# Down products of two SwiGLU layers: eight of 22 row pairs as seven block products in three of the four column halves

## The chip, the cores and the metric

The kernel is one program on one core of one Trainium2 chip. The metric is the device time of one execution in microseconds (us); each kernel is given as the median of its runs.

## What is computed

A decoder layer on a sequence of 256 rows of width 2048, all float32: a half-step SwiGLU, a mixing layer (a recurrent one and a gated linear one side by side), a second half-step SwiGLU, a final norm. The change concerns the two SwiGLU layers alone, and in them the last product, `@ w_down`.

```python
D_FF = 11 * D_MODEL // 4        # 5632
def swiglu(x, w_gate, w_up, w_down):
    return (jax.nn.silu(x @ w_gate) * (x @ w_up)) @ w_down

h = h + 0.5 * swiglu(rms_norm(h, ffn1_norm[l]), ffn1_w_gate[l], ffn1_w_up[l], ffn1_w_down[l])
...                             # mixing layer
h = h + 0.5 * swiglu(rms_norm(h, ffn2_norm[l]), ffn2_w_gate[l], ffn2_w_up[l], ffn2_w_down[l])
return rms_norm(h, final_norm)
```

## The kernel before, in words

Every float32 operand is split into a rounded part and a rest (`hi`, `lo`), and a product is three matmuls: hi by hi, hi by lo, lo by hi (`three`, lines 156 to 158). For a weight the split is made on the fly: one 1 MB transfer, issued by SyncE (line 134), brings a **pair** of row tiles (256 rows by 1024 columns) into a buffer `wst`; ScalarE casts 1024 elements per partition into `whi` (line 116) and VectorE subtracts them into `wlo` (line 117).

The down product of a layer runs over two **pieces**, the column halves of `w_down`. In each piece the 5632 rows of `w_down` are 22 pairs, and `DOWN_PLAN` says in one letter each how a pair is multiplied:

- **n**, plain: two row tiles by two row blocks of the output by two column blocks, 8 block products, 24 matmuls of 512 columns. Two casts and two subtractions of 1024 elements.
- **S**, shared: the 2 by 2 blocks are combined as in Strassen's and Winograd's schemes, 7 block products, 21 matmuls. VectorE first forms sums of weight blocks into a second buffer `t` (lines 143, 144, 145), and then `b11,b21` (one split of 1024), `b22` (one of 512), `t1,t3` and `t2,t4` (1024 each) are split. The sums of the other side, the hidden activations `hT`, are made beforehand (`block_sums`, and `earlier_sums` for pairs whose activations stand early).

Buffers decide how far ahead the weights can be prepared. `wst`, `whi` and `wlo` have three buffers each (pool `wpool`, `bufs=3`), `b22` has one of its own. A buffer is handed out again in turn and is waited for until its last reader is done. In the gate and up products the sums `t` of an S lie in a separate room; in the down products (`core.room = None`) `t` takes one of the three `wst` buffers, so an S takes two of the three. With n, S and t handed out in turn, "nnS" repeated moves the buffers on by one each time, while in "nS" repeated an S gets the buffer of the S before it, and an n that of the n before it.

The order on each engine is fixed when the program is built, by priorities; a row that waits holds up all behind it on that engine, and SyncE issues its transfers in order too.

Of the kernel before, what the change touches and what calls it, by code (L numbers as in the profile page):

```python
# [12 lines left out]
F32 = mybir.dt.float32  # L13
F32R = mybir.dt.float32r
# [3 lines left out]
P = 128  # L18
# [244 lines left out]
        nc.vector.reciprocal(rstd, tmp)  # L263


def ffn(core, xhi, xlo, rstd, wg, wu, wd, after_first, after_down, fpool, down, rest, back, spare, more, head=None):
    nc, NT, NK, D, S = core.nc, core.NT, core.NK, core.D, core.S
    DFF = wg.shape[1]
    NF = DFF // P
# [89 lines left out]
    for c0, w in chunks:  # L359
        if c0:  # L360
            own, aux = ([core.bank(i) for i in b] for b in (range(4), range(4, 8)))
            sg = fpool.tile([P, NT, 1024], F32, name=core.name("sg"), tag="sg")
            last_s = GATE_PLAN.rindex("S")
            hooks = {last_s: [lambda: shared(aux, sg)]}
# [32 lines left out]
        sg = scrap  # L397
# [11 lines left out]
        pending = [lambda c0=c0, w=w, hid=hid: hidden_T(c0, w, hid)]  # L409
    core.room = None  # L410
    back()
    four, (hraw, two) = spare(), more()
    first_s = NF // 2 - 6
    hsums = lambda p: four(p) if p >= NF // 2 - 4 else tuple(two[:, i, p - first_s, :] for i in range(2))

    def earlier_sums():

        for n, p in enumerate(range(first_s, first_s + 2)):
            pair = slice(2 * p, 2 * p + 2)
            nc.vector.tensor_tensor(hraw[:, n], hT_hi[:, pair, :].bitcast(F32), hT_lo[:, pair, :].bitcast(F32), ALU.add)  # L420
            block_sums(hraw[:, n], *hsums(p))

    for piece, (c0, w) in enumerate(down):
        own, aux = ([core.bank((4 * piece + i) % 8) for i in b] for b in (range(4), range(4, 8)))
        plan = DOWN_PLAN[piece]
        number = {"n": iter(range(first_s)), "S": iter(range(first_s, NF // 2))}
        ids = [next(number[kind]) for kind in plan]
        hooks = {}
        if piece == 0:
            hooks[0] = [earlier_sums]  # L430
            hooks[DOWN_HIDDEN_AT] = [partial(f, sums=hsums) for f in pending]
        tmp = lambda: fpool.tile([P, NT, 1024], F32, name=core.name("dsh"), tag="hid")
        hooks[plan.rindex("S")] = [lambda: shared_h(aux, tmp(), c0)]
        core.rows_times_pairs(wd, c0, plan, ids, own, aux, hT_hi, hT_lo, hsums, hooks)
        for n in range(2):
            for t in range(NT):
                hs = core.h[:, t, c0 + n * 512 : c0 + (n + 1) * 512]
                nc.vector.scalar_tensor_tensor(hs, own[2 * t + n], 0.5, hs, ALU.mult, ALU.add)
            after_down(piece, n)
# [676 lines left out]
NSLOT = 17  # L1116
GATE_PLAN, UP_PLAN = "nSnSnSnn", "nSnSnSnn"
HIDDEN_AT = 6
DOWN_PLAN, DOWN_HIDDEN_AT = ("nnnnSnnSnnSnnSnnSnnSnn", "nnSnnSnnSnnSnnSnnSnnnn"), 2


@with_exitstack
def kernel(ctx: ExitStack, tc: tile.TileContext, dram: dict, out: bass.AP):
    nc = tc.nc
    x = dram["x"][0]
    S, D = x.shape
    core = Core(ctx, tc, S, D, 1024)
    const, NK = core.const, core.NK
    HD = D // 2
# [7 lines left out]
    rstd = [const.tile([P, core.NT], F32, name=f"rstd{i}") for i in range(4)]  # L1137
# [8 lines left out]
    def norm_half(i, hf, xhi, xlo):  # L1146
        core.transposed(hf * NK // 2, NK // 2, gT[:, i * NK : (i + 1) * NK], xhi, xlo, (0, 1, 2, 3) if hf == 0 else (4, 5, 6, 7))

    def norm_rows(i, bank, pool):
        for hf in range(2):  # L1150
            core.sumsq(hf * HD, HD, ssq[i][hf], pool)
        core.rstd_of(ssq[i][:2], rstd[i])
        if bank is not None:
            core.spread_rstd(rstd[i], bank)
# [14 lines left out]
    with ExitStack() as front:  # L1169
        xa, xa_half, xa_sums, xa_pool = xt_pool(front, "xa")  # L1170
        with ExitStack() as st:
            hpool = st.enter_context(tc.tile_pool(name="h1", bufs=1))
            fpool = st.enter_context(tc.tile_pool(name="ffn1", bufs=1))
            core.h = hpool.tile([P, core.NT, D], F32, name="h1", tag="h")
            with tc.high_priority(offset=9000):
                load_gain(0, fpool, nc.scalar)
            for q in range(4):
                with tc.high_priority(offset=(9000, 8600, 8400, 8300)[q]):
                    cs = slice(q * 512, (q + 1) * 512)
                    nc.sync.dma_start(out=core.h[:, :, cs], in_=x[:, cs].rearrange("(t p) d -> p t d", p=P))  # L1180

            def norm_quarter(q):
                core.transposed(4 * q, 4, gT[:, :NK], *xa, ((2, 3), (4, 5), (6, 7))[q % 3])

            with tc.high_priority(offset=8800):
                norm_quarter(0)

            def first_norm():
                with tc.issue_after(core.last_split.ins):
                    norm_rows(0, 7, fpool)  # L1190
                for i in (1, 2):
                    load_gain(i, fpool, nc.sync)

            def rest():
                return hpool.tile([P, core.NT, D], F32, name="wsums1", tag="h")

            def back():
                core.h = hpool.tile([P, core.NT, D], F32, name="h1b", tag="h")
                for hf in range(2):
                    cs = slice(hf * HD, (hf + 1) * HD)  # L1200
                    nc.sync.dma_start(out=core.h[:, :, cs], in_=x[:, cs].rearrange("(t p) d -> p t d", p=P))

            def more():

                raw = xa_pool.tile([P, 4, 2, S], F32, name="hsum1", tag="lo0")
                return raw, fpool.tile([P, 2, 2, 512], F32R, name="hsum1b", tag="sg")

            def park(hf, n):
                if n == 0:
                    return  # L1210
                for n, v in zip(("hi", "lo"), xa):
                    v.tiles[hf] = xa_half(n, hf)
                norm_half(1, hf, *xa)
                if hf == 1:
                    norm_rows(1, 6, fpool)
                nc.sync.dma_start(out=parked[hf], in_=core.h[:, :, hf * HD : (hf + 1) * HD])

            ffn(core, *xa, rstd[0], dram["ffn1_w_gate"][0], dram["ffn1_w_up"][0], dram["ffn1_w_down"][0],
                first_norm, park, fpool, [(0, HD), (HD, HD)], rest, back, xa_sums, more, head={q: partial(norm_quarter, q + 1) for q in range(3)})
        mix_layer(core, dram, *xa, scratch, NSLOT)  # L1220
        right = dict(side="right", reuse_waits="tile")
        h2 = ctx.enter_context(tc.tile_pool(name="h2", bufs=1, **right))

        def back2():
            core.h = h2.tile([P, core.NT * D + 24], F32, name=core.name("h2"), tag="h")[:, : core.NT * D].rearrange(
                "p (t d) -> p t d", t=core.NT)
            for hf in range(2):
                nc.sync.dma_start(out=core.h[:, :, hf * HD : (hf + 1) * HD], in_=parked[hf])

        back2()  # L1230
        xb, _, xb_sums, xb_pool = xt_pool(ctx, "xb", **right)

        def half_done(hf):
            norm_half(2, hf, *xb)
            nc.sync.dma_start(out=parked[hf], in_=core.h[:, :, hf * HD : (hf + 1) * HD])

        mix_out(core, dram["w_out"][0], *xa, half_done)
    with ExitStack() as st:
        fpool = st.enter_context(tc.tile_pool(name="ffn2", bufs=1, reuse_waits="tile"))
        down = [(0, HD), (HD, HD)]  # L1240
        fb = None

        def more2():
            raw = xb_pool.tile([P, 4, 2, S], F32, name="hsum2", tag="lo0")
            return raw, xb_pool.tile([P, 2, 2, 512], F32R, name="hsum2b", tag="hi0")

        def closing(piece, n):
            nonlocal fb
            if piece == 0 and n == 0:
                return  # L1250
            if piece == 0:
                with tc.issue_after(core.last_silu.ins):
                    nc.scalar.activation(warm, ssq[0][0], AF.Sqrt)
                fb = fpool.tile([P, D], F32, name="final_gain", tag="sg")
                nc.sync.dma_start(out=fb, in_=dram["final_norm"].rearrange("(o d) -> o d", o=1).broadcast_to([P, D]))
            c0, w = ((0, HD), (HD, HD // 2), (HD + HD // 2, HD // 2))[piece + n * piece]
            core.sumsq(c0, w, ssq[3][piece + n * piece], fpool)
            for t in range(core.NT):
                hs = core.h[:, t, c0 : c0 + w]
                nc.vector.tensor_tensor(hs, hs, fb[:, c0 : c0 + w], ALU.mult)  # L1260

        def rest2():
# [2 lines left out]

        warm = const.tile([P, core.NT], F32, name="warm")
        ffn(core, *xb, rstd[2], dram["ffn2_w_gate"][0], dram["ffn2_w_up"][0], dram["ffn2_w_down"][0],
            lambda: norm_rows(2, 7, fpool), closing, fpool, down, rest2, back2, xb_sums, more2)
        core.rstd_of(ssq[3], rstd[3])
        for hf in range(2):  # L1270
            for t in range(core.NT):
# [34 lines left out]
```

## Time and profile before

| | |
|---|---|
| median of 3 runs | 1915.48 us (1914.80 to 1916.83) |
| profiled execution: its own time | 1916.29 us |
| span of that execution, first to last instruction | 1914.6 us |
| granted TensorE clock, mean | 0.994 of full speed |
| TensorE (PE) busy | 1881.2 us, 98% |
| VectorE (DVE) busy | 1575.3 us, 82% |
| ScalarE (ACT) busy | 1036.2 us, 54% |

The span and the profiled execution's own time differ by 1.7 us, which lies outside the first and last instruction. Times in rows are us from the start of the span. PE rows of matmuls overlap: the distance between two starts is what one costs.

### The profile page before, as it was taken

The page shows a single profiled execution, that of the slowest core. Times are in us where ns is not written, and L with a number is a line of the kernel's source. Part 1 is how long each engine was busy: PE and PEld are TensorE (multiplying, and loading weights), DVE is VectorE, ACT ScalarE, POOL GpSimd, SP SyncE. Part 2 cuts the span into 40 slices and gives each one's busy share as a digit, 9 for nine tenths or more (in the row PEclk, how much of TensorE's full clock was granted, in tenths as well). Part 3 has the DMA queues.
Part 4 walks back from the last instruction along what each step waited for, and adds up shares of the span by engine and source line. Part 5 has one row for each costly group of instructions (what it writes and reads, how often), then busy time and mean ns, then how long its engine had stood idle before and what let it go on. Part 6 is the DMA issues. An engine that isn't in the chain of part 4 may idle for free.

```text
span 1914.6 us, 25771 instructions
## 1 busy us (share of the span) xinstructions
PE 1881.2 (98%) x10161; PEld 1583.4 (83%) x10161; DVE 1575.3 (82%) x2044; ACT 1036.2 (54%) x1261; POOL 9.6 (1%) x53
## 2 busy tenths in 40 slices
PE   7999999999999999999999999999999999999997
PEld 6888888888888889898899978888878888888886
DVE  6889899898978776986595775988898989987876
ACT  6555555655555555543454554665655555554553
POOL 0000000000000001000000000000000000000000
PEclk9999999999999999998999999999999999999999
DMA  6556555655556566545243456655655555656664
GB/s 224 194 188 208 179 214 181 215 187 210 199 199 227 203 204 213 179 122 152 79 145 118 126 200 204 206 209 178 217 179 200 195 198 197 240 185 203 213 204 141
DMA packets 124401, 360.77 MB, mean 188 GB/s; under 512 B 20879, under 2 KB 23128, under 8 KB 124152
## 3 DMA queue, kind: packets, MB, share of 16 engines
q1 hardware_dynamic: 123960, 358.08, 55.6%
q8 instruction: 79, 1.29, 0.3%
q10 hardware_dynamic: 320, 1.06, 0.1%
q14 instruction: 42, 0.34, 0.1%
HBM read 351.25 MB, written 7.86 MB: 188 GB/s over the span
## 4 chain that ended last, share of the span: by engine, by line
PE 89%; DVE 5%; DMA 3%; ACT 2%; issue 1%; SPq 0%; DVEq 0%; ACTq 0%
PE bank L157 21%; PE bank L158 21%; PE bank L156 21%; PE bank L205 4%; PE bank L206 4%; PE bank L207 4%; PE bank L196 3%; PE bank L194 3%; PE bank L193 3%; DMA wst<-in_ffn_w_up_dram 2%; DVE wlo L117 1%; DVE wlo L98 1%; PE bank L286 1%; PE bank L781 1%; DMA wst<-in_ffn_w_gate_dram 1%
## 5 line engine op out<-in xcount | busy, mean ns | idle before, releaser
L116 ACT CAST whi<-wst 128x1024 fp32r<-128x1024 f32 (+1 forms) x544 | 528.6, 987 | 419.5 <-PE bank L158 374.4
L117 DVE TENSOR_TENSOR wlo<-wst,whi 128x1024 fp32r<-128x1024 f32 (+1 forms) x544 | 610.0, 1137 | 87.6 <-ACT whi L116 78.9
L157 PE MATMUL bank<-wlo,hThi 128*128 128x512 f32 x824 | 322.1, 391 | 1.7 <-DVE wlo L117 1.7
L156 PE MATMUL bank<-whi,hThi 128*128 128x512 f32 x824 | 320.8, 389 | 0.0
L158 PE MATMUL bank<-whi,hTlo 128*128 128x512 f32 x824 | 320.8, 389 | 0.0
L97 ACT CAST whi<-wst 128x1024 fp32r<-128x1024 f32 (+2 forms) x153 | 157.6, 1032 | 185.2 <-PE bank L206 105.0
L98 DVE TENSOR_TENSOR wlo<-wst,whi 128x1024 fp32r<-128x1024 f32 (+2 forms) x153 | 182.6, 1195 | 91.2 <-ACT whi L97 90.6
L116 ACT CAST whi<-wsums 128x1024 fp32r<-128x1024 f32 x120 | 126.5, 1055 | 165.0 <-PE bank L158 142.5
L205 PE MATMUL bank<-xahi,whi 128*128 128x256 f32 x688 | 199.6, 290 | 3.7 <-DVE raw L639 3.7
L206 PE MATMUL bank<-xalo,whi 128*128 128x256 f32 x688 | 198.0, 288 | 0.0
L207 PE MATMUL bank<-xahi,wlo 128*128 128x256 f32 x688 | 197.8, 288 | 0.0
L157 PE MATMUL bank<-wlo,xbhi 128*128 128x512 f32 x490 | 191.6, 391 | 0.2 <-DVE wlo L117 0.2
L157 PE MATMUL bank<-wlo,xahi 128*128 128x512 f32 x490 | 191.6, 391 | 0.0
L158 PE MATMUL bank<-whi,xblo 128*128 128x512 f32 x490 | 190.9, 390 | 0.0
L158 PE MATMUL bank<-whi,xalo 128*128 128x512 f32 x490 | 190.8, 389 | 0.0
L156 PE MATMUL bank<-whi,xbhi 128*128 128x512 f32 x490 | 190.0, 390 | 0.0
L156 PE MATMUL bank<-whi,xahi 128*128 128x512 f32 x490 | 190.0, 390 | 0.0
L157 PEld LDWEIGHTS bank<-wlo,hThi 128*128 128x128 f32 x824 | 154.7, 188 | 38.2 <-DVE wlo L117 6.3
L156 PEld LDWEIGHTS bank<-whi,hThi 128*128 128x128 f32 x824 | 154.6, 188 | 32.0
L158 PEld LDWEIGHTS bank<-whi,hTlo 128*128 128x128 f32 x824 | 154.7, 188 | 31.4
L117 DVE TENSOR_TENSOR wlo<-wsums,whi 128x1024 fp32r<-128x1024 f32 x120 | 146.2, 1221 | 38.3 <-ACT whi L116 36.8
L205 PEld LDWEIGHTS bank<-xahi,whi 128*128 128x128 f32 x688 | 133.2, 194 | 7.8 <-DVE raw L639 3.9
(355 smaller groups left out, 2699.3 us busy)
## 6 DMA issues: line engine op xcount, KB each, us to landing
wst<-in_ffn_w_up_dram SPq DMA_DIRECT2D x88, 1024.0 KB, 5.1
wst<-in_ffn_w_down_dram SPq DMA_DIRECT2D x88, 1024.0 KB, 5.5
wst<-in_ffn_w_gate_dram SPq DMA_DIRECT2D x87, 1024.0 KB, 5.7
wst<-in_w_in_dram SPq DMA_DIRECT2D x40, 1024.0 KB, 5.4
wst<-in_w_out_dram SPq DMA_DIRECT2D x16, 1024.0 KB, 6.3
h<-parked SPq DMA_DIRECT2D x4, 1024.0 KB, 7.7
wst<-in_w_in_dram SPq DMA_DIRECT2D x4, 640.0 KB, 5.2
h<-in_x_dram SPq DMA_DIRECT2D x4, 512.0 KB
```

Of the source, the lines that this page charges most:

```text
L97: self.last_split = nc.scalar.copy(hi[:, : m * width], src)
L98: nc.vector.tensor_tensor(lo[:, : m * width], src, hi[:, : m * width].bitcast(F32), ALU.subtract)
L116: self.nc.scalar.copy(hv, src)
L117: self.nc.vector.tensor_tensor(lv, src, hv.bitcast(F32), ALU.subtract)
L156: nc.tensor.matmul(out, a[0], b[0], start=first, stop=False)
L157: nc.tensor.matmul(out, a[0], b[1], start=False, stop=False)
L158: self.last_mm = nc.tensor.matmul(out, a[1], b[0], start=False, stop=last)
L193: nc.tensor.matmul(banks[t][n][:, :w], a, whi[:, c : c + w], start=first, stop=False)
L194: nc.tensor.matmul(banks[t][n][:, :w], a, wlo[:, c : c + w], start=False, stop=False)
L205: nc.tensor.matmul(out, a, xhi[:, k, :], start=first, stop=False, skip_group_check=True)
L206: nc.tensor.matmul(out, a, xlo[:, k, :], start=False, stop=False, skip_group_check=True)
L207: nc.tensor.matmul(out, b, xhi[:, k, :], start=False, stop=last, skip_group_check=True)
```

## The change

In three of the four pieces the number of S pairs goes from six to eight: both pieces of the second layer and the first of the first layer (`EIGHT_FIRST`, `EIGHT_LAST`). The last piece of the first layer keeps six (`SIX_LAST` is the old plan). The S pairs are always the last ones by number, 14 to 21 now, 16 to 21 before. The plans before were `nnnnSnnSnnSnnSnnSnnSnn` (first piece) and `nnSnnSnnSnnSnnSnnSnnnn` (last piece).

The activation sums of the two added pairs (14 and 15) need a place: in the first layer a tile in the first half of `x`, which no product reads any more, in the second layer the gate's tile `sg`. The final gain, which was loaded into `sg`, is loaded into the tile of the raw sums (`lo0`).

```diff
-    four, (hraw, two) = spare(), more()
-    first_s = NF // 2 - 6
-    hsums = lambda p: four(p) if p >= NF // 2 - 4 else tuple(two[:, i, p - first_s, :] for i in range(2))
-    def earlier_sums():
-        for n, p in enumerate(range(first_s, first_s + 2)):
+    four, (hraw, *twos) = spare(), more()
+    def hsums(p):
+        n = NF // 2 - 5 - p
+        return four(p) if n < 0 else tuple(twos[n // 2][:, i, n % 2, :] for i in range(2))
+    def earlier_sums(*ps):
+        for p in ps:
+            n = NF // 2 - 5 - p
             pair = slice(2 * p, 2 * p + 2)
             nc.vector.tensor_tensor(hraw[:, n], hT_hi[:, pair, :].bitcast(F32), hT_lo[:, pair, :].bitcast(F32), ALU.add)
             block_sums(hraw[:, n], *hsums(p))
...
-        plan = DOWN_PLAN[piece]
+        plan = down_plan[piece]
+        first_s = NF // 2 - plan.count("S")
...
         if piece == 0:
-            hooks[0] = [earlier_sums]
+            for n in range(2):
+                hooks[n] = [partial(earlier_sums, first_s + 2 * n, first_s + 2 * n + 1)]
...
-DOWN_PLAN, DOWN_HIDDEN_AT = ("nnnnSnnSnnSnnSnnSnnSnn", "nnSnnSnnSnnSnnSnnSnnnn"), 2
+EIGHT_FIRST, EIGHT_LAST, SIX_LAST = "nnnnSnSnSnnSnSnSnSnSnn", "nnSnSnSnnSnSnSnSnSnnnn", "nnSnnSnnSnnSnnSnnSnnnn"
+DOWN_HIDDEN_AT = 2
...
-                return raw, fpool.tile([P, 2, 2, 512], F32R, name="hsum1b", tag="sg")
+                return (raw, fpool.tile([P, 2, 2, 512], F32R, name="hsum1b", tag="sg"),
+                        xa_pool.tile([P, 2, 2, 512], F32R, name="hsum1c", tag="hi0"))
...
-            return raw, xb_pool.tile([P, 2, 2, 512], F32R, name="hsum2b", tag="hi0")
+            return (raw, xb_pool.tile([P, 2, 2, 512], F32R, name="hsum2b", tag="hi0"),
+                    fpool.tile([P, 2, 2, 512], F32R, name="hsum2c", tag="sg"))
...
-                fb = fpool.tile([P, D], F32, name="final_gain", tag="sg")
+                fb = xb_pool.tile([P, D], F32, name="final_gain", tag="lo0")
```

What it does to the order is shown at three places. On VectorE, in the steady part of the second layer's first piece, before: one S (buffer `wst_2398`, its sums in `wst_2399`) with the two subtractions of the n ahead of it and the first of the n behind it.

```order
L143 TENSOR_TENSOR wst_2399_14927<-wst_2398_14925 128x1024
L117 TENSOR_TENSOR wlo_2403_14936<-wst_2398_14925,whi_2402_14935 128x512
L117 TENSOR_TENSOR wlo_2397_14898<-wst_2393_14891,whi_2396_14897 128x1024
L144 TENSOR_TENSOR wst_2399_14927<-wst_2399_14927,wst_2398_14925 128x512
L145 TENSOR_TENSOR wst_2399_14927<-wst_2398_14925,wst_2399_14927 128x512
L117 TENSOR_TENSOR wlo_2401_14932<-wst_2398_14925,whi_2400_14931 128x1024
L117 TENSOR_TENSOR wlo_2405_14940<-wst_2399_14927,whi_2404_14939 128x1024
L117 TENSOR_TENSOR wlo_2407_14944<-wst_2399_14927,whi_2406_14943 128x1024
L117 TENSOR_TENSOR wlo_2410_14971<-wst_2408_14968,whi_2409_14970 128x1024
```

The same piece in the change, one S (`wst_2423`, sums in `wst_2424`) of those that follow each other with one n between:

```order
L117 TENSOR_TENSOR wlo_2420_14994<-wst_2418_14991,whi_2419_14993 128x1024
L143 TENSOR_TENSOR wst_2424_15027<-wst_2423_15025 128x1024
L117 TENSOR_TENSOR wlo_2422_14998<-wst_2418_14991,whi_2421_14997 128x1024
L144 TENSOR_TENSOR wst_2424_15027<-wst_2424_15027,wst_2423_15025 128x512
L117 TENSOR_TENSOR wlo_2426_15032<-wst_2423_15025,whi_2425_15031 128x1024
L145 TENSOR_TENSOR wst_2424_15027<-wst_2423_15025,wst_2424_15027 128x512
L117 TENSOR_TENSOR wlo_2428_15036<-wst_2423_15025,whi_2427_15035 128x512
L117 TENSOR_TENSOR wlo_2430_15040<-wst_2424_15027,whi_2429_15039 128x1024
L117 TENSOR_TENSOR wlo_2432_15044<-wst_2424_15027,whi_2431_15043 128x1024
```

Of the rows that read the S's weights, the last is now the `b22` row of 512 (`wlo_2428`), seven rows into the S; the second subtraction of the n ahead (`wlo_2422`) stands behind line 143 as before.

On SyncE's queue at the same place, before (2378, 2398 and 2418 are S, the others n; each S comes behind two n):

```order
L134 DMA wst_2378_14814<-in_ffn2_w_down_dram 128x2x1024 [waits DMAHW3_49,DVE_49]
L134 DMA wst_2388_14857<-in_ffn2_w_down_dram 128x2x1024 [waits DMAHW7_49,DVE_49]
L134 DMA wst_2393_14891<-in_ffn2_w_down_dram 128x2x1024 [waits DMAHW0_49,DVE_49]
L134 DMA wst_2398_14925<-in_ffn2_w_down_dram 128x2x1024 [waits DMAHW6_49,DVE_49]
L134 DMA wst_2408_14968<-in_ffn2_w_down_dram 128x2x1024 [waits DMAHW2_49,DVE_49]
L134 DMA wst_2413_15002<-in_ffn2_w_down_dram 128x2x1024 [waits DMAHW3_49,DVE_49]
L134 DMA wst_2418_15036<-in_ffn2_w_down_dram 128x2x1024 [waits DMAHW1_49,DVE_49]
```

and in the change (2368 and 2373 are n, 2378 is the first S of five, then n and S in turn):

```order
L134 DMA wst_2368_14726<-in_ffn2_w_down_dram 128x2x1024 [waits DMAHW3_49,DMAHW1_49,DVE_49]
L134 DMA wst_2373_14760<-in_ffn2_w_down_dram 128x2x1024 [waits DMAHW2_49,DMAHW4_49,DVE_49,Activation_49]
L134 DMA wst_2378_14794<-in_ffn2_w_down_dram 128x2x1024 [waits DVE_49]
L1263 DMA final_gain_15228<-in_final_norm_dram 128x2048 [waits DVE_49,PE_49]
L134 DMA wst_2388_14837<-in_ffn2_w_down_dram 128x2x1024 [waits DMAHW4_49,DVE_49]
L134 DMA wst_2393_14871<-in_ffn2_w_down_dram 128x2x1024 [waits DMAHW5_49,DVE_49]
L134 DMA wst_2403_14914<-in_ffn2_w_down_dram 128x2x1024 [waits DMAHW7_49,DVE_49]
L134 DMA wst_2408_14948<-in_ffn2_w_down_dram 128x2x1024 [waits DMAHW0_49,DVE_49,Activation_49]
```

The S transfers now stand one n apart. The load of the final gain, which was issued behind the first S of the piece (`wst_2318`, four n ahead of it), is now issued behind the fourth (`wst_2378`), ahead of the n behind that.

Near the start of the first layer's first piece, VectorE in the change (`wst_751` is the second S, `hsum1`, `hTlo` and `xasum` belong to the last chunk of activations, which is still being transposed and summed there):

```order
L117 TENSOR_TENSOR wlo_748_4152<-wst_746_4149,whi_747_4151 128x1024
L143 TENSOR_TENSOR wst_752_4185<-wst_751_4183 128x1024
L117 TENSOR_TENSOR wlo_756_4194<-wst_751_4183,whi_755_4193 128x512
L117 TENSOR_TENSOR wlo_750_4156<-wst_746_4149,whi_749_4155 128x1024
L144 TENSOR_TENSOR wst_752_4185<-wst_752_4185,wst_751_4183 128x512
L308 TENSOR_TENSOR hsum1_3875<-hsum1_3875 128x128
L145 TENSOR_TENSOR wst_752_4185<-wst_751_4183,wst_752_4185 128x512
L294 TENSOR_TENSOR hTlo_9_139<-bank_730_4058,hThi_8_138 128x512
L117 TENSOR_TENSOR wlo_754_4190<-wst_751_4183,whi_753_4189 128x1024
L311 TENSOR_TENSOR xasum_703_3874<-hsum1_3875,xasum_702_3873 128x512
```

Before, an n stood in this place between the same activation rows, and the second S came after it.

## Rows read from the trace of the kernel before

**Rows 1.** The page: busy time and share of each engine; granted clock in 40 slices.

```profile
PE 1881.2 (98%) x10161; PEld 1583.4 (83%) x10161; DVE 1575.3 (82%) x2044; ACT 1036.2 (54%) x1261; POOL 9.6 (1%) x53
...
PEclk9999999999999999998999999999999999999999
```

**Rows 2.** The page: chain that ended last, share of the span by engine.

```profile
PE 89%; DVE 5%; DMA 3%; ACT 2%; issue 1%; SPq 0%; DVEq 0%; ACTq 0%
```

**Rows 3.** Waits of PE: us in total, times, longest.

```profile
PE bank L157 <- DVE wlo L117: 1.9, 5, 0.7
```

**Rows 4.** Windows: first piece of the first and of the second layer.

```profile
495.00:613.00 118.00, 117.99 (x533) 97.69 (x532) 96.24 (x115) 64.07 (x74) 0.00 (x0) 1.00 0.54 195
...
1682.00:1791.00 109.00, 108.96 (x490) 90.13 (x489) 89.34 (x107) 60.43 (x69) 0.00 (x0) 1.00 0.59 194
```

**Rows 5.** Timeline of PE: start, length; an n, then an S.

```profile
1753.14 0.39 PE L156 MATMUL bank<-whi,hThi 128*128 128x512 f32 x1
...
1755.86 0.39 PE L156 MATMUL bank<-whi,hThi 128*128 128x512 f32 x1
...
1757.22 0.39 PE L156 MATMUL bank<-whi,xbsum 128*128 128x512 f32 x1
```

**Rows 6.** Timeline of VectorE: the second S of the second layer's first piece.

```profile
1701.08 1.23 DVE L143 TENSOR_TENSOR wst<-wst 128x1024 f32<-128x1024 f32 x1 [0.22 <-DMA wst<-in_ffn_w_down_dram]
1702.22 2.35 DVE L117 TENSOR_TENSOR wlo<-wst,whi 128x1024 fp32r<-128x1024 f32 x2
1704.49 0.68 DVE L144 TENSOR_TENSOR wst<-wst,wst 128x512 f32<-128x512 f32 x1
1705.10 1.22 DVE L117 TENSOR_TENSOR wlo<-wst,whi 128x1024 fp32r<-128x1024 f32 x1
1706.23 0.69 DVE L145 TENSOR_TENSOR wst<-wst,wst 128x512 f32<-128x512 f32 x1
1706.84 0.68 DVE L117 TENSOR_TENSOR wlo<-wst,whi 128x512 fp32r<-128x512 f32 x1
```

**Rows 7.** Timeline of SyncE: issues of 1 MB transfers; the length is the issue's.

```profile
549.10 0.37 SPq L134 DMA_DIRECT2D wst<-in_ffn_w_down_dram  x1
...
1695.58 0.37 SPq L134 DMA_DIRECT2D wst<-in_ffn_w_down_dram  x1
...
1707.58 0.37 SPq L134 DMA_DIRECT2D wst<-in_ffn_w_down_dram  x1
...
1735.91 0.37 SPq L134 DMA_DIRECT2D wst<-in_ffn_w_down_dram  x1
...
1738.37 0.37 SPq L134 DMA_DIRECT2D wst<-in_ffn_w_down_dram  x1
...
1742.80 0.37 SPq L134 DMA_DIRECT2D wst<-in_ffn_w_down_dram  x1
```

**Rows 8.** Timelines of VectorE and ScalarE: rows that start when a transfer lands.

```profile
554.05 1.23 DVE L143 TENSOR_TENSOR wst<-wst 128x1024 f32<-128x1024 f32 x1 [0.25 <-DMA wst<-in_ffn_w_down_dram]
...
1748.80 1.23 DVE L143 TENSOR_TENSOR wst<-wst 128x1024 f32<-128x1024 f32 x1 [1.13 <-DMA wst<-in_ffn_w_down_dram]
...
1745.36 1.05 ACT L116 CAST whi<-wst 128x1024 fp32r<-128x1024 f32 x1 [0.49 <-DMA wst<-in_ffn_w_down_dram]
```

**Rows 9.** Issues by window: 495 to 613, 1682 to 1791, 1791 to 1906; last, median us to landing.

```profile
wst<-in_ffn_w_down_dram SPq DMA_DIRECT2D x21, 1024.0 KB, 5.1
...
wst<-in_ffn_w_down_dram SPq DMA_DIRECT2D x20, 1024.0 KB, 5.6
...
wst<-in_ffn_w_down_dram SPq DMA_DIRECT2D x19, 1024.0 KB, 6.2
```

**Rows 10.** Timeline of ScalarE: the cast of `b11,b21`, and what it waited for.

```profile
1750.62 1.06 ACT L116 CAST whi<-wst 128x1024 fp32r<-128x1024 f32 x1 [0.31 <-PE bank L158]
```

**Rows 11.** Timeline of SyncE: the load of the final gain.

```profile
1675.39 0.35 SPq L1255 DMA_DIRECT2D final_gain<-in_final_norm_dram  x1
```

**Rows 12.** Timelines of VectorE: one addition of 512 and one of 128 elements.

```profile
476.03 0.68 DVE L420 TENSOR_TENSOR hsum<-hThi,hTlo 128x512 f32<-128x512 f32 x1
476.63 0.28 DVE L306 TENSOR_TENSOR hsum<-hsum 128x128 f32<-128x128 f32 x1
476.83 0.28 DVE L305 TENSOR_TENSOR hsum<-hsum 128x128 f32<-128x128 f32 x1
```

**Rows 13.** Groups of PE, 500 to 545: the transposes; count, busy us, mean ns.

```profile
L286 PE MATMUL bank<-ident,hid 128*128 128x128 f32 x16 | 1.9, 273 | 0.0
```

**Rows 14.** Windows: the start of the first layer's first piece (DVE is the third number).

```profile
475.00:507.00 32.00, 32.00 (x142) 26.48 (x142) 29.42 (x41) 15.88 (x17) 0.00 (x0) 1.00 0.68 246
507.60:540.00 32.40, 32.39 (x152) 26.69 (x151) 28.10 (x43) 21.88 (x28) 0.00 (x0) 1.00 0.56 195
```

More of the change, by code (lines that the diff above doesn't have):

```diff
@@ L263, in rstd_of, with ffn @@
         nc.vector.reciprocal(rstd, tmp)
-def ffn(core, xhi, xlo, rstd, wg, wu, wd, after_first, after_down, fpool, down, rest, back, spare, more, head=None):
+def ffn(core, xhi, xlo, rstd, wg, wu, wd, after_first, after_down, fpool, down, rest, back, spare, more, down_plan, head=None):
     nc, NT, NK, D, S = core.nc, core.NT, core.NK, core.D, core.S
@@ L1218 @@
             ffn(core, *xa, rstd[0], dram["ffn1_w_gate"][0], dram["ffn1_w_up"][0], dram["ffn1_w_down"][0],
-                first_norm, park, fpool, [(0, HD), (HD, HD)], rest, back, xa_sums, more, head={q: partial(norm_quarter, q + 1) for q in range(3)})
+                first_norm, park, fpool, [(0, HD), (HD, HD)], rest, back, xa_sums, more, (EIGHT_FIRST, SIX_LAST), head={q: partial(norm_quarter, q + 1) for q in range(3)})
         mix_layer(core, dram, *xa, scratch, NSLOT)
@@ L1267 @@
         ffn(core, *xb, rstd[2], dram["ffn2_w_gate"][0], dram["ffn2_w_up"][0], dram["ffn2_w_down"][0],
-            lambda: norm_rows(2, 7, fpool), closing, fpool, down, rest2, back2, xb_sums, more2)
+            lambda: norm_rows(2, 7, fpool), closing, fpool, down, rest2, back2, xb_sums, more2, (EIGHT_FIRST, EIGHT_LAST))
         core.rstd_of(ssq[3], rstd[3])
```

## The prediction, as it was made before the run

> **What bounds the kernel now.** The page's engine shares come first [rows 1]: TensorE (PE) is busy 98% of the span, at the higher of its two clock levels nearly throughout, and the chain that ended last is 89% PE [rows 2]. So work taken from PE counts in full as long as PE doesn't begin to wait. Its waits for this kind of weight are next to nothing now: the largest kind, on `wlo`, comes to 1.9 us in five waits [rows 3], and in two of the three pieces that change PE is busy 117.99 of 118.00 and 108.96 of 109.00 us [rows 4]. VectorE has some 18% of these stretches free, the DMA engines 41 to 46% [rows 4]. By averages there is room; what decides is the time that one S needs from its transfer's issue to the next one's.
>
> **What is saved.** Two matmuls stand 226.7 ns apart: 1753.14 to 1757.22 is 18 of them [rows 5]. An n (24) takes 5.44 us, an S (21) 4.76, "nS" 10.2, "nnS" 15.64. Six pairs become S, each three matmuls less: 18 by 0.2267 is 4.1 us.
>
> The Trainium skill ("TensorE: Matmul & The Clock Gate", section "Back-to-back issue gap") puts a matmul of 512 columns in a real stream at some 131 ns; the saving would then be 2.4 us, an estimate from that page. The rows give 226.7 ns and decide.
>
> **What is added: a loop.** An S takes two of the three `wst` buffers. In "nS" repeated, its transfer can only be issued once the previous S has read its own weights for the last time, so from S to S runs a chain: transfer, VectorE's rows on it, next issue. Its VectorE part stands in the trace [rows 6]: line 143 at 1701.08, two subtractions from 1702.22 (one is the n's ahead), line 144, `b11,b21`, line 145, `b22`, and the next issue at 1707.58 [rows 7], 6.5 us behind the landing. In "nnS" there are two subtractions of 1.14 us in front, in "nS" the order shows one: 5.4 us.
>
> The other part is the transfer, issue to landing, D. Alone: 1695.58 to 1701.08, 5.5 us; issued 4.43 us behind another (1738.37 to 1742.80): 1742.80 to 1748.73 (ScalarE's row) or 1748.80, 5.9; the one issued at 1738.37, itself 2.5 behind one at 1735.91, landed at 1745.36, 7.0 [rows 7, 8]. Medians are 5.6 and 6.2 us in the second layer's pieces, 5.1 in the first layer's, where one took 549.10 to 554.05, 4.95 [rows 7 to 9]. In "nS" the S's transfer is issued behind the `b22` row, the n's behind the n's second subtraction, so the n's is ahead by 0.61 + 1.14 + 0.61 + 0.61, 3.0 us: two in flight. That is nearest to the 5.9; I take **D = 6.0** in the second layer and, by the same step from the median, 5.2 in the first.
>
> The loop is then 5.4 + 6.0 = 11.4 us in the second layer, where PE needs 10.2, and 10.6 in the first. Chains are short, so a lead is used up first. Let l be the S's landing less the start on PE of the n ahead of it. In front of S on VectorE's queue stands line 143, which waits for the transfer, and behind it the n's second subtraction, which PE wants 12 matmuls (2.72 us) into the n, one more (0.23) for the `wlo` operand. 2.95 less 1.14, 1.22 and about 0.2 for hand-overs: PE waits once l is over 0.4. The next issue comes at l + 5.4, but not before some 3.8: the cast of `b11,b21` needs a buffer freed at the n's start (1750.62 against 1750.42, [rows 10], one n ahead of 1755.86 in [rows 5]), and the rows behind it follow. Thus l of the next is max(3.8, l + 5.4) + D - 10.2. The first S behind two n landed at 1748.73, l = -1.7, before; since its buffers now come from an S chain that ran with less lead I take -1.2.
>
> With D = 6.0: the second S has l = 0.0, the third 1.2, a wait of 0.8; each further S, starting from 0.4, has l = D - 4.4 = 1.6, a wait of 1.2. A chain of three S costs 0.8, of five 0.8 + 1.2 + 1.2 = 3.2. Each of the second layer's two pieces has one of each: 2 by 4.0 = **8.0 us**. With D = 5.2 (first layer) l goes -0.8, -0.4, 0, 0.4: no wait. Its steady first chain is hidden by that lead; were D 5.75 there, the piece would wait 2.5.
>
> **The final gain.** Its 1 MB load, at 1675.39 before, four n ahead [rows 11], now stands on SyncE's queue behind the first S of five, ahead of an n, in the stretch where leads are used up. A third transfer in flight raised D by about 1 (7.0 against 5.9); half of that lands on the chain: **+0.5** (0 to 1.0).
>
> **VectorE at a piece's start.** While the last chunk of activations is transposed and summed, two more S's rows crowd in. From line 143 of the first S to the third S's last subtraction the order counts 18 rows of 1024 elements, 18 of 512 and 16 of 128: by 1.14, 0.61 and 0.20 us (starts in [rows 6, 12]) 34.7 us. PE's three n, three S and transposes (1.9, [rows 13]) take 32.5. The sums for two more pairs, 2 by (0.6 + 4 by 0.2 + 0.6) = 4.0 us, fall where VectorE is busy 29.4 of 32.0 and 28.1 of 32.4 us already [rows 14]. The lead of the four n ahead hides most of it; I take **+0.7** a layer (0 to 2.3), 1.4 in all.
>
> Everything else is equal: same bytes of weights, ScalarE with over 40% free, no other row moved past these stretches.
>
> **The sum.** 8.0 + 0.5 + 1.4 - 4.1 = +5.8 us. On the profiled execution's own 1916.29 (span 1914.6 and 1.7 around it) that is 1922.1; that execution is 0.8 above the median of 1915.48, so the forecast for the median is **1921.3 us**, 0.3% slower. Bounds: with D = 5.5 a chain of five waits 1.2, of three 0, so 2.4 - 4.1 = -1.7, 1913.8. With D = 6.4 chains wait 4.8 and 1.6: 12.8 + 0.5 + 1.4 - 4.1 = +10.6, 1926.1, or 1928.6 with the first layer's 2.5. With D = 7.0: 20 + 2.5 + 4.6 + 0.5 - 4.1 = +23.5, 1939.
>
> **Rivals.**
>
> *Waits and saving cancel.* D stays near 5.5 as for the lone transfer, or the lead lasts longer than I take it: waits of 2 to 6 us, 1914 to 1918. For it: the DMA engines are little more than half busy [rows 4] and bytes per us hardly rise. Against it: at D = 5.5 the loop is still 10.9.
>
> *The other side: the loop is hidden.* If D is 4.8 or less the loop is under 10.2 us; no chain waits, and the time is 1915.5 - 4.1 = 1911.4. For it: the row of 4.95 us. Against it: that is the first layer's, and both medians of the second layer lie above 5.5 [rows 9]. The Trainium skill ("DMA: Bandwidth & Descriptors", section "Anatomy of one DMA — SWDGE (gpsimd) path") fits a transfer as 2.0 us and its bytes at 436 GB/s: 4.4 us for 1 MB, an estimate from that page, by which the loop would be 9.8 and this rival would come true. The rows, from SyncE's queue, show 4.95 to 7.0 and none that short, so it gets little weight.
>
> *The chip shares badly.* Two and three transfers in flight take 6.4 to 7.0 each, as the one at 1738.37 did, and VectorE falls behind at both starts: +11 to +24, 1926 to 1939. Against it: that transfer was issued 2.5 us behind another, closer than 3.0.
>
> **How the numbers follow.** A difference of about 0.2% (3.8 us) is what a measurement of this kernel can tell from none. Chances: the loop binds in the second layer alone, D 5.7 to 6.4 (1917 to 1926), 0.60; cancelling 0.22; hidden 0.07; bad sharing 0.11. Of the first case some 0.08 lies within 0.2%, of the second 0.21 does and 0.01 is below; the third is faster, the last slower. So faster 0.08, same 0.29, slower 0.63. The range leaves out the hidden case and the upper part of the last: 1914.5 to 1928.5.
>
> **What would show it.** Right: in the second layer's chains of five S PE waits on `wlo` of line 117 and `whi` of line 116, about 1.2 us for each "nS", whose period is 11.4; line 143 waits for its transfer; SyncE issues in turn some 3 and 8.4 us apart; D there is about 6; the first layer's piece shows PE without waits and about 1.4 us shorter less what its start loses; 10143 matmuls in all. Wrong: a period of 10.2 with D at 5.6 or under (the lead or the VectorE part was mis-sized), or waits that stand at the piece starts and not in the chains.

## The result and the profile after

The changed kernel takes 1925.28 us (median of 4 runs, 1923.93 to 1926.53) against 1915.14 us (1914.16 to 1916.83) for the kernel before on the same chip: ratio 1.0051, interval 1.0040 to 1.0063. It is slower by 10.1 us. The forecast was 1921.3 us, in a range of 1914.5 to 1928.5: the side and the place are right, the loss is nearly twice as large as forecast.

The page of the changed kernel: busy time, clock, and the chain that ended last by engine.

```profile
PE 1885.7 (98%) x10143; PEld 1581.4 (82%) x10143; DVE 1603.3 (83%) x2098; ACT 1046.5 (54%) x1277; POOL 9.7 (1%) x53
...
PEclk9999999999999999999998999999999999999999
...
PE 80%; DVE 9%; DMA 7%; ACT 2%; issue 1%; SPq 0%; DVEq 0%; ACTq 0%
```

PE runs 18 matmuls fewer, as forecast, at nearly the same mean granted clock (0.992 of full speed, 0.994 before). Its share of the chain has fallen from 89% to 80%, VectorE's has risen from 5% to 9% and the transfers' from 3% to 7% [rows 1, 2]: the engine that set the end now waits. The profiled execution's own time is 1926.53 us, its span 1924.8.

PE's waits in the changed kernel: total, times, longest.

```profile
PE bank L157 <- DVE wlo L117: 7.3, 16, 0.9
```

Five waits of 1.9 us have become sixteen of 7.3 [rows 3]. The same question for the second layer's down product alone, from 1686 to 1913 us, gives fourteen of them, where the kernel before has none:

```profile
PE bank L157 <- DVE wlo L117: 6.1, 14, 0.9
```

Where they lie is seen in PE's rows. In the second layer's first piece, the first row of each S that reads a `sum`:

```profile
1742.27 0.39 PE L156 MATMUL bank<-whi,xbsum 128*128 128x512 f32 x1
...
1754.15 0.39 PE L156 MATMUL bank<-whi,xbsum 128*128 128x512 f32 x1
...
1765.76 0.39 PE L156 MATMUL bank<-whi,xbsum 128*128 128x512 f32 x1
```

"nS" takes 11.9 and 11.6 us where its 45 matmuls take 10.2 [rows 5]. The two waits inside the first of these periods, one in each half of the n:

```profile
1746.40 0.50 PE L157 MATMUL bank<-wlo,hThi 128*128 128x512 f32 x1 [0.34 <-DVE wlo L117]
...
1750.15 0.50 PE L157 MATMUL bank<-wlo,hThi 128*128 128x512 f32 x1 [0.71 <-DVE wlo L117]
```

What these waits hang on is told by the chain that ended last, asked for the stretch from 1738 to 1768 us alone: first the shares by line, then the pieces in order of time (start, length). A piece that reaches over an edge of the stretch counts in full, so the shares add up to more than 100%.

```profile
by line: DMA wst<-in_ffn_w_down_dram 63.6%; DVE wlo L117 29.1%; DVE wst L143 8.2%; DVE wst L145 6.0%; DVE wst L144 6.0%; issue 0.8%; SPq L134 0.2%; DVEq L143 0.1%
...
1741.19 6.45 DMA wst<-in_ffn_w_down_dram
...
1747.74 1.23 DVE wst L143
1748.96 1.14 DVE wlo L117
1750.10 0.60 DVE wst L144
1750.70 1.14 DVE wlo L117
1751.84 0.60 DVE wst L145
1752.44 0.61 DVE wlo L117
...
1753.10 6.12 DMA wst<-in_ffn_w_down_dram
...
1764.69 6.52 DMA wst<-in_ffn_w_down_dram
```

This is the loop of the prediction, piece for piece: transfer, line 143, the n's second subtraction, 144, `b11,b21`, 145, `b22`, next issue. From landing to issue it takes 5.5 us (1747.64 to 1753.10); PE does not appear in it at all. In the first layer's piece, from 545 to 580 us, the same question gives PE alone:

```profile
by line: PE bank L158 33.7%; PE bank L157 33.6%; PE bank L156 33.1%
```

Below, a kernel's **second stretch** is the time from the first transpose of the second layer's first down piece (line 286) to the start of PE's last matmul, its **first stretch** that from the same transposes in the first layer's first down piece to the first transpose of line 235 (of `h1b`), about where that piece ends; where lines moved, their copies are meant. Both lie in one execution. Two rows bound the second stretch after:

```profile
1686.39 1.91 PE L286 MATMUL bank<-ident,hid 128*128 128x128 f32 x16
...
1912.73 0.39 PE L158 MATMUL bank<-whi,hTlo 128*128 128x512 f32 x1
```

226.34 us; before it was 216.75. The first stretch went from 101.39 to 100.31. So the change costs 9.59 - 1.08 = 8.5 us there. The other 1.6 us of the difference lie in stages whose code is the same. From the last down matmul of the first layer to the first transposes of the second layer's hidden activations, with the mixing layer between them, PE took 551.2 us before and 554.4 after (549.5 to 551.5 in all later profiles); the remaining stages were 1.6 us shorter after. The longer time in the middle is TensorE's clock. Windows of the changed kernel and then of the one before; the third number from the end is the granted clock:

```profile
1025.00:1035.00 10.00, 10.00 (x94) 9.71 (x93) 3.65 (x3) 3.49 (x7) 0.00 (x0) 0.50 0.02 5
...
1025.00:1035.00 10.00, 10.00 (x169) 9.46 (x168) 5.73 (x4) 5.46 (x9) 0.00 (x0) 1.00 0.29 101
```

After, PE ran at the lower of its two levels (1.2 GHz) for 10.2 us from 1024.9 us on, behind 10 us in which it was busy throughout. No other profile here has such a stretch at this place, and over it PE fell 4.4 us behind. Whether the three unprofiled executions had it too is not known.

Where PE's distances from start to start exceed 0.2267 us, the excess sums in the second stretch to 12.3 us after and 0.4 before. That is twice the idle time of 6.1 us: PE's rows overlap by 0.16 us, which a wait takes up before PE is idle, the row behind a wait starts another 0.11 late, and delays too short to leave PE idle make up the rest. After, by place: piece starts 0.42 (before 0.40), chains of three S 0.25 and 1.18, chains of five 5.53 and 4.94.

### The profile page after: what moved, and what is told of

Same layout as the page of the kernel before. It is cut to its first block, busy times and chain, and to the rows that moved or that the text cites. A ratio compares the mean times of both kernels' runs of the same rounds, so it can differ in the third digit from the quotient of the medians.

```text
span 1924.8 us, 25808 instructions
## 1 busy us (share of the span) xinstructions
PE 1885.7 (98%) x10143; PEld 1581.4 (82%) x10143; DVE 1603.3 (83%) x2098; ACT 1046.5 (54%) x1277; POOL 9.7 (1%) x53
## 4 chain that ended last, share of the span: by engine, by line
PE 80%; DVE 9%; DMA 7%; ACT 2%; issue 1%; SPq 0%; DVEq 0%; ACTq 0%
PE bank L157 18%; PE bank L158 18%; PE bank L156 18%; DMA wst<-in_ffn_w_down_dram 4%; DVE wlo L117 4%; PE bank L205 4%; PE bank L206 3%; PE bank L207 3%; PE bank L194 3%; PE bank L196 3%; PE bank L193 3%; DMA wst<-in_ffn_w_up_dram 2%; DVE wlo L98 1%; PE bank L286 1%; PE bank L786 1%
## 5 line engine op out<-in xcount | busy, mean ns | idle before, releaser
L116 ACT CAST whi<-wst 128x1024 fp32r<-128x1024 f32 (+1 forms) x556 | 536.4, 983 | 417.1 <-PE bank L158 337.4
L117 DVE TENSOR_TENSOR wlo<-wst,whi 128x1024 fp32r<-128x1024 f32 (+1 forms) x556 | 619.9, 1132 | 65.8 <-ACT whi L116 58.9
L157 PE MATMUL bank<-wlo,hThi 128*128 128x512 f32 x794 | 312.2, 393 | 7.8 <-DVE wlo L117 7.3
L156 PE MATMUL bank<-whi,hThi 128*128 128x512 f32 x794 | 309.4, 390 | 0.0
L158 PE MATMUL bank<-whi,hTlo 128*128 128x512 f32 x794 | 309.4, 390 | 0.0
L157 PEld LDWEIGHTS bank<-wlo,hThi 128*128 128x128 f32 x794 | 149.0, 188 | 50.0 <-DVE wlo L117 19.4
L156 PEld LDWEIGHTS bank<-whi,hThi 128*128 128x128 f32 x794 | 149.0, 188 | 31.5 <-ACT whi L116 0.4
L158 PEld LDWEIGHTS bank<-whi,hTlo 128*128 128x128 f32 x794 | 149.1, 188 | 29.6
```

Source lines behind the costliest of these rows:

```text
L116: self.nc.scalar.copy(hv, src)
L117: self.nc.vector.tensor_tensor(lv, src, hv.bitcast(F32), ALU.subtract)
L156: nc.tensor.matmul(out, a[0], b[0], start=first, stop=False)
L157: nc.tensor.matmul(out, a[0], b[1], start=False, stop=False)
L158: self.last_mm = nc.tensor.matmul(out, a[1], b[0], start=False, stop=last)
```

## The experiments

Times are medians of 10 to 12 runs, ratios go with the kernel before on the same chip in the same hours (1914.3, 1915.8 and 1915.2 us in the three groups, medians of 34, 33 and 23 runs). Single runs of any one kernel spread over 4 to 12 us, so the stretches carry what lies under 2 us. Each is read from one profile; the change and e6, whose loops are the same, differ by 1.2 us in the second.

**Theory:** the loop through the S's buffer. **Rivals:** VectorE is too full with two more S per piece; transfers are slower because of what else moves (the final gain above all); the start of a piece is what costs.

### e1: eight S in the first layer alone

```diff
-            ... more2, (EIGHT_FIRST, EIGHT_LAST))
+            ... more2, (SIX_FIRST, SIX_LAST))
```

> Eight S in the first layer's first piece alone; the second layer has six in both pieces again, with all else as in the change. Loop theory (an S waits for the previous S's buffer; it binds only where a transfer takes over 5 us): the first layer's transfers take 4.9 us, so its piece keeps its gain; the trace of the change gave 1.1 us there. 1914.0 us against 1915.1 before (1913.5 to 1915). Rival (VectorE is too full, above all at a piece's start): the piece loses what it gains, 1915 to 1917.

The sums made early are cut to the number of S. 1913.2 us, ratio 1.000 (0.9992 to 1.0009). First stretch 100.31, as in the change; second 216.81, as before. So the whole loss is the second layer's. The gain of 1.1 us is there in the stretch and too small for the times.

### e2: the sums in another room

```diff
+        if self.room is None and self.apart:
+            return self.bpool.tile([P, 2 * self.WMAX], F32, name=self.name("sums"), tag="hid")
         if self.room is None:
             return self.wpool.tile(... tag="wst")
...
+            self.apart = p - first_s >= 1
```

> All eight S kept, but from the second S of a piece on the sums t lie in the room that the hidden chunk leaves free, and no longer in one of the three wst buffers. VectorE's rows are the same in number and length. Loop theory: S and n then take one buffer each, transfers are issued an S earlier, the waits on wlo in the chains of five go: about 12 us of waits of the second layer less 1 to 2 at its start, so 1925.3 - 10.5 = 1914.8 (1911 to 1916.5). Rival (VectorE too full): the waits stay, since its work stays: 1922 to 1926.

1914.6 us, ratio 1.0004 (0.9993 to 1.0016); second stretch 220.28. VectorE does the same rows, and the waits in the chains of five are gone but for some 0.15 us in each nS. So VectorE's load isn't the cause. Most of what remains stands at the start, where the change has hardly any waits: the second S's sums go there into the room that the hidden chunk is only just leaving. PE's waits between 1680 and 1730 us:

```profile
PE bank L161 <- ACT hsum L304: 1.6, 1, 1.6
PE bank L162 <- DVE wlo L118: 1.4, 1, 1.4
```

These rows tell where PE waits, not that the room is the reason; e9 asks for that.

### e3: another order on VectorE, the same buffers

```diff
-        self.nc.vector.tensor_tensor(lv, src, hv.bitcast(F32), ALU.subtract)
+        self.last_lo = self.nc.vector.tensor_tensor(lv, src, hv.bitcast(F32), ALU.subtract)
...
-                    nc.vector.tensor_tensor(t[:, 0:2], b[:, :, 1, :], b[:, 0], ALU.subtract)
+                    behind = self.tc.issue_after(self.last_lo.ins) if self.room is None else nullcontext()
+                    with behind:
+                        nc.vector.tensor_tensor(t[:, 0:2], b[:, :, 1, :], b[:, 0], ALU.subtract)
```

> The buffers as in the change; only the order on VectorE differs: line 143, which waits for the S's transfer, is queued behind the second subtraction of the n ahead of it. Loop theory: the loop loses one row of 1.14 us and PE no longer waits for a subtraction queued behind the landing: 4.3 + 6.3 = 10.6 us against PE's 10.2, which the lead covers in a chain of five: 1925.3 - 9 = 1916 (1913 to 1919). Rival (VectorE too full): same rows, same time, 1923 to 1927. Rival (a wait takes the other's place: line 143 late, so b11,b21 late): 1920 or more.

1910.7 us, ratio 0.9981 (0.9972 to 0.9991), better than the expected 1913 to 1919; second stretch 216.49. The edit asks for one row's place on VectorE's queue. Every engine does the same rows; a few others moved along (`b11,b21` now stands ahead of line 144, and some rows of ScalarE and PE changed places). 9.85 us came back, where the change had lost 9.59. The timeline of VectorE in this kernel (line 145 is the change's 143):

```profile
1743.25 1.22 DVE L117 TENSOR_TENSOR wlo<-wst,whi 128x1024 fp32r<-128x1024 f32 x1
1745.42 1.23 DVE L145 TENSOR_TENSOR wst<-wst 128x1024 f32<-128x1024 f32 x1 [0.95 <-DMA wst<-in_ffn_w_down_dram]
1746.56 1.22 DVE L117 TENSOR_TENSOR wlo<-wst,whi 128x1024 fp32r<-128x1024 f32 x1
```

VectorE still waits for the landing, but the n's subtraction that PE wants first is now done ahead of that wait, and the loop is a row shorter: 4.3 us from the landing (1745.33) to the next S's issue (1749.65). The expectation overlooked a second gain, which SyncE's rows show (an S, an n, an S):

```profile
1739.84 0.37 SPq L134 DMA_DIRECT2D wst<-in_ffn_w_down_dram  x1
...
1744.49 0.37 SPq L134 DMA_DIRECT2D wst<-in_ffn_w_down_dram  x1
...
1749.65 0.37 SPq L134 DMA_DIRECT2D wst<-in_ffn_w_down_dram  x1
```

Since the n's subtraction no longer waits for the S's landing, the transfers go out 4.7 to 5.3 us apart and no longer 3.0 and 8.9. Each then takes 5.4 to 5.6 us, where the S's took 6.2. So the loop is some 9.8 us, under PE's 10.2, and not the 10.6 that was expected.

### e4: the S spread

```diff
-EIGHT_FIRST, EIGHT_LAST, SIX_LAST = "nnnnSnSnSnnSnSnSnSnSnn", "nnSnSnSnnSnSnSnSnSnnnn", ...
+EIGHT_FIRST, EIGHT_LAST, SIX_LAST = "nnnnSnSnnSnSnSnnSnSnSn", "nnSnSnnSnSnnSnSnnSnSnn", ...
```

> Eight S as in the change, spread so that S, n, S, n stand in chains of two, three and three (first pieces: nnnnSnSnnSnSnSnnSnSnSn) and two by two (last piece: nnSnSnnSnSnnSnSnnSnSnn) in place of three and five. Loop theory: with a transfer of 6.2 us a chain of two costs nothing, one of three 1.0 to 1.5: 1925.3 - 12.3 + 3 + 0.7 = 1916.7 (1914 to 1919). Rival (VectorE too full over the piece as a whole): as many S, as much work, 1923 to 1927.

1918.6 us, ratio 1.0026 (1.0017 to 1.0035), second stretch 221.98. Shorter chains, smaller loss, with as much work: for the loop, against a full VectorE. More stays than expected: two n between chains win one n's 5.44 us, yet PE still waits in the chains behind them (0.7 us at 1761.64, 0.8 at 1858.74), so they do not restore the lead, the time by which an S's weights land ahead of need.

### e5: the second layer reads the first layer's matrix

```diff
-        ffn(core, *xb, rstd[2], ... dram["ffn2_w_down"][0],
+        ffn(core, *xb, rstd[2], ... dram["ffn1_w_down"][0],
```

> The change with one name altered: the second layer's down product reads the first layer's w_down (so another product is computed). Every queue's order and every row is the same. In both traces so far a transfer alone takes 4.9 us in the first layer's pieces and 5.5 to 5.6 in the second layer's, the one issued 3.0 us behind it 4.9 to 5.0 and 6.2. If that goes with the matrix, the second layer's transfers become 4.9 and the loop 10.3 us: the waits in the chains of five go, and the second layer from its last transposes to PE's end falls from 226 us to some 216 (1925 - 10 = 1915; 1913 to 1918). If it goes with the place in the program (what else moves there), the transfers stay at 5.6 and 6.2 and the time at 1923 to 1926.

1914.8 us, ratio 0.9995 (0.9987 to 1.0004), second stretch 216.03. Issues of the changed kernel and then of this one, each from 1687 to 1795 and from 1795 to 1905 us; the last number is the median to landing:

```profile
wst<-in_ffn_w_down_dram SPq DMA_DIRECT2D x20, 1024.0 KB, 5.6
...
wst<-in_ffn_w_down_dram SPq DMA_DIRECT2D x19, 1024.0 KB, 5.7
```

```profile
wst<-in_ffn_w_down_dram SPq DMA_DIRECT2D x21, 1024.0 KB, 4.9
...
wst<-in_ffn_w_down_dram SPq DMA_DIRECT2D x17, 1024.0 KB, 4.9
```

The order on every queue is that of the change, the transfers are 0.7 to 0.8 us shorter, and 10 us are gone. So the transfer's time is the loop's other half, and it goes with the matrix that is read, not with the place in the program. Why the second layer's `w_down` takes longer is not shown by these runs.

### e6: without the final gain's load

```diff
-                fb = xb_pool.tile([P, D], F32, name="final_gain", tag="lo0")
-                nc.sync.dma_start(out=fb, in_=dram["final_norm"]...)
...
-                nc.vector.tensor_tensor(hs, hs, fb[:, c0 : c0 + w], ALU.mult)
+                nc.vector.tensor_tensor(hs, hs, hs, ALU.mult)
```

> The change without the load of the final gain (the scaling multiplies h by itself, so the last norm is another). The prediction put 0.5 us (0 to 1.0) on this load: the second layer's stretch 226.3 would be 225.3 to 226.3; a fall of more than 1.5 would mean that the third transfer was under-sized.

One run, 1925.0 us; second stretch 227.50, above the expected 225.3 to 226.3 and not shorter than the change's 226.34. So the load costs nothing that shows: the S's transfer ahead of it took 6.15 us here and 6.51 with it, but what follows differs by more between the two profiles.

### e9: the sums apart from the fourth S on

```diff
+            self.apart = p - first_s >= (3 if plan[:4] == "nnnn" else 1)
```

> As e2, but in the first pieces only from the fourth S on (the chain of five), so that no sum at a piece's start waits until the hidden chunk is transposed. Loop theory: the chain-of-five waits of the first pieces are gone as in e2, those of the chain of three stay, the 4 us that e2 lost at the second layer's start come back: its stretch 226.3 in the change, 220.3 in e2, falls to some 217, the time to 1911 to 1914. Rival (the waits of e2 at the start are VectorE's load from the two more S, whatever room): it stays at 220 and 1914 to 1916.

Second stretch 217.53, as expected: 2.75 us of what e2 lost came back with the same rows on VectorE, so it was the room and not VectorE's load. The time, 1916.3 us and ratio 1.0001 (0.9991 to 1.0010), does not show it: the expected 1911 to 1914 was missed.

### e11: the kernel before with e3's order

> The kernel before with e3's order alone: line 143 queued behind the second subtraction of the n ahead of it, still six S. Loop theory: in nnS there is no loop that binds, PE waits 2 us in all there, so nothing or at most 1 us is won: 1913.5 to 1915 beside 1914.3 before. Rival (e3's gain comes from the order and owes nothing to eight S): 1910 to 1912, as e3.

1914.0 us, ratio 0.9989 (0.9980 to 0.9998); stretches 101.25 and 216.60, against 101.39 and 216.75 before. In the stretches the order alone gives 0.3 us, as it should where no loop binds. The times say 0.1% more than that; so a ratio of 0.999 is about what unchanged stages can bring about here.

### e12: e3 with the gain's load behind the piece's last transfers

```diff
-                nc.sync.dma_start(
+                self.last_load = nc.sync.dma_start(
                     out=st.rearrange("p (k f) -> p k f", k=2),
...
+                with tc.issue_after(core.last_load.ins):
                     nc.sync.dma_start(out=fb, in_=dram["final_norm"]...)
```

> e3 with the final gain's load queued behind the last transfers of the piece, no longer between the fourth S and the n behind it. In e3 PE waits 0.75 us for a subtraction of the S behind that load and 0.4 on the n before. If the load is the cause (a third transfer in flight), the second layer's stretch falls from 216.5 to 215.4 and the time by 1 us against e3 (1909.7). If it is the lead that the chain of three has used up, the waits stay and so does the time (1910.7).

1915.1 us, ratio 0.9996 (0.9987 to 1.0005), second stretch 217.14 against 216.49 in e3. The wait of 0.75 us stayed where it was. So the load was not its cause; that the lead is, only the other of the two expected cases says. A new wait of 0.5 us came up late in the piece, at 1779.18: the load is now issued at 1770.65, between two transfers issued at 1770.24 and 1773.70, and these took 7.3 and 8.8 us. The time lost more than the stretch: 0.9996 against e3's 0.9981 is some 3 us, of which the stretch has 0.65.

### e10 and e13: both cures together

e10 joins e9, e3 and e12. In e13, with e3's order too, the gain is loaded as in the change and the sums are apart from the third S on:

```diff
+            self.apart = p - first_s >= (2 if plan[:4] == "nnnn" else 1)
```

> e9's room for the sums, e3's order on VectorE and e12's place of the gain together. e9 still has some 0.15 us in every nS at the n's second half, where the subtraction queued behind line 143 comes late: with that order turned these go. Loop theory: what is left is the chain of three with shared buffers and the start: the second layer's stretch 215.3, against 216.5 in e3 and 217.5 in e9, and the time 1.5 to 4 us under the kernel before (0.998 to 0.999). Rival (the small waits are casts that wait for PE's buffers): the stretch stays at 216.5 to 217.5 and the time within 1 us of the kernel before.

> As e10, but with the sums apart from the third S on in the first pieces (e9 and e10: the fourth), and the gain loaded where the change loads it. If the third S's sums need not wait for the hidden chunk's room, the first chain has one shared step less: stretch 214.5 to 215, time 0.998. If they do wait, as the second's did in e2, the stretch is 217 or more.

e10: 1912.3 us, ratio 0.9985 (0.9974 to 0.9995). e13: 1913.2 us, ratio 0.9983 (0.9973 to 0.9993). Both have a second stretch of 214.20 us (e10 was expected at 215.3), 2.55 less than before, where the 12 matmuls saved there are worth 2.72; the first stretches are 100.15 and 100.17, 1.2 less, of 1.36. Asked for 1738 to 1768 us, the chain of e13 is PE alone again:

```profile
by line: PE bank L163 34.0%; PE bank L164 33.3%; PE bank L165 33.1%
```

So the saving is real, and 3.8 us of the 4.1 are to be had once neither the buffer nor the place of line 143 ties an S to the one before it.

## Why the prediction was right, and where it was off

- **The saving** (18 matmuls by 0.2267, 4.1 us): right. e10 and e13 bring 3.8 of it to light.
- **The loop:** right in mechanism and in each piece. Landing to issue was put at 5.4 us and measured 5.5; e2 and e9 (buffer), e3 (order, and with it the transfers' spacing) and e5 (transfer) each take one part of it away, and each time most of the chains' waits go. Two details differ: in the second layer's stretch PE never waited on `whi`, and it waited in both halves of the n, where the prediction reckoned with the second alone.
- **The first layer has no waits:** right. Its second transfers take 4.9 to 5.0 us (5.2 was taken), the stretch is 1.08 us shorter.
- **The step that was mis-sized is the 8.0 us for the chains, which measured 11.9.** D was taken as 6.0, by the 5.9 of a transfer 4.4 us behind another; at the 3.0 us of this loop it was 6.45, 6.12 and 6.52 in the rows above, 6.2 to 6.3 in the medians of the two pieces' 13. With D = 6.25 the prediction's own formula gives 4.2 for a chain of five and 1.3 for one of three, 11.0 in all: 3 of the 3.9 us that were missing. A nearer transfer stood in the trace before: issued at 1707.58 [rows 7], 2.98 us behind the one at 1704.60, it landed at 1713.73, 6.15 us later.
- **The rest of the 3.9 us is the lead.** In the first piece the first S of five landed 0.9 us ahead of its n's start (1.2 was taken). The second was issued at 1729.36 and landed at 1735.27, 0.3 us behind the start of its n, where 0.0 was taken. At 0.3 PE was still to be without a wait, yet it waited 0.42: on ScalarE the n's second cast stood behind the `b22` cast that waits for the S's landing, a queue of which the prediction said nothing; in that round landing to issue was 5.9 us. Round by round the chain of five in the first piece cost 0, 0.42, 1.6, 1.3 and 1.7 us, and 0.4 in the n behind it, where 0, 0, 0.8, 1.2 and 1.2 were forecast; 5.5 and 4.9 in the two pieces for 3.2 each. Those of three, 0.25 and 1.18 for 0.8 each, were right on average.
- **The final gain, +0.5:** not to be seen (e6). Its source was misread: no third transfer was in flight around 1738.37, since the one from 1735.91 had landed at 1741.46, ahead of the issue at 1742.80. Nor did the change put the load into the tight stretch: it was issued at 1718.09 and landed at 1726.44, and the next weights were issued only then. What a third transfer costs is seen late in e12.
- **VectorE at the piece starts, +1.4:** nearly nothing. The second layer's start costs PE 0.42 us after and 0.40 before; the first layer's stretch misses 0.28 of its 1.36. The four n ahead hide the rest.
- The two wrong terms, 1.9 us too much, made up for half of the 3.9 too little. The remaining 1.6 us of the measured 10.1 lie in unchanged stages, where in the profiled execution the clock alone took 4.4, and are no part of the explanation.
- **Rivals:** "waits and saving cancel" needed a transfer near 5.5, "hidden" one of 4.8 or less: e5 tests this at one point. With 4.9 to 5.0 the second stretch is 0.7 us under before, so most of the waits are hidden; the whole saving there would be 2.7. A transfer of 5.5 at this spacing no run shows. "Shares badly" wanted 6.4 to 7.0 each: with 6.2 for an S's transfer and a change of 10.1 us the result stands just short of it.
- **The Trainium skill's rules:** by "DMA: Bandwidth & Descriptors", section "Anatomy of one DMA — SWDGE (gpsimd) path", the loop would have been hidden; the measured transfers, 4.9 and 5.6 us alone, lie above the 4.4 estimated from it. By "TensorE: Matmul & The Clock Gate", section "Back-to-back issue gap", 18 matmuls would be 2.4 us, an estimate from that page; the stretches of e10 and e13 give 3.8, near the 4.1 of 226.7 ns each.

What stays open: why one matrix is read more slowly than the other, whether the clock's stretch in the mixing layer is in every execution of the change, and how much of the ratios between 0.998 and 0.999 is the order and how much the spread of the unchanged stages.

## What to carry to other kernels

A step that saves work on the bound engine can be worth less than nothing when it takes a second buffer of a ring: follow the ring round once, from a transfer's issue to the issue that waits for the same buffer, and compare that time with the engine's time for the same work. A row that waits for a transfer should stand on its queue behind the rows that are ready and wanted first; here one row's place was worth 9.85 us with eight S, and 0.3 with six (e11), where no loop binds. Such a place also sets when the next transfers are issued, and so how far they overlap. And a lead that one long chain has used up does not come back in one spare step.

## What the runs showed of the hardware

- The same 1 MB transfer, alone on the queue, takes 4.9 us from the first layer's `w_down` and 5.5 to 5.6 us from the second layer's, as medians of every kernel here (5.1 for the first in the kernel before). It goes with the matrix: read in the second layer's place (e5), the first layer's takes 4.9 there too.
- In the changed kernel a second transfer issued 3.0 us behind the first took about as long as the first in the first layer (both 4.9 us, now and then 5.2) and some 0.7 longer in the second (5.6 and 6.2): there 2.6 us of the first were left when the second was issued, in the first layer 1.9. In e2 and e4, with 2.5 us left, the second took 5.7. Issued 4.7 to 5.3 us apart (e3), transfers took 5.4 to 5.6.
- A matmul that had to wait costs 0.11 us beyond its wait: the row after it starts 0.34 us later and not 0.23 (1746.40 to 1746.74 in the changed kernel, and so behind each such wait).
- A stretch of 10.2 us at the lower level of TensorE's clock (0.50 in the rows above) set PE back by 4.4 us against the same rows of the kernel before.
